# A FFN–mixer–FFN layer on one core: plain last chunk by token block, x normalised while the modulation's weights load

## The chip, the core and the metric

The kernel runs on one core of a Trainium2 chip. The metric is the device time of one execution in microseconds (us); the time before is the median of three runs. The profile is one execution recorded by the hardware profiler. The engines are called PE (TensorE: matmuls; PEld: its weight loads), DVE (VectorE), ACT (ScalarE), POOL (GpSimd) and SP, whose queue issues all DMAs of this kernel in order. PSUM is the memory that PE writes, SBUF the one that all engines read, and DRAM lies off the core.

## The reference

One layer over 1024 latent tokens `x` and 256 context tokens `ctx`, width 1024. The two streams have modulations of their own, from `c` and `c_ctx`.

```python
def rmsnorm(x, g):
    n = x * lax.rsqrt(jnp.mean(x * x, axis=-1, keepdims=True) + EPS)
    return n * g

def swiglu(y, w_in, w_out):
    gate, up = jnp.split(y @ w_in, 2, axis=-1)
    return (jax.nn.silu(gate) * up) @ w_out

m_x = (silu(c) @ w_ada + b_ada).reshape(9, 1024)          # m_c from c_ctx
x = x + 0.5 * m_x[2] * swiglu(rmsnorm(x, g1) * (1 + m_x[1]) + m_x[0], ff1_in, ff1_out)
h = h + 0.5 * m_c[2] * swiglu(rmsnorm(h, g1) * (1 + m_c[1]) + m_c[0], ff1_in, ff1_out)
# mixer: gated linear attention (GLA) and a gated MLP (gMLP) share one input and one output projection;
# the latent scans start from the context's states
x = x + m_x[5] * mix_x
x = x + 0.5 * m_x[8] * swiglu(rmsnorm(x, g3) * (1 + m_x[7]) + m_x[6], ff2_in, ff2_out)
return rmsnorm(x, final_g)
```

The hidden width of an FFN is 2816, that is 22 tiles of 128.

## The kernel before

All tensors stand transposed: channels on the 128 partitions, tokens along the free axis. `x[k][tb]` is channel tile k (8 of them) of token block tb: blocks 0 and 1 have 512 latent tokens each, block 2 is the context with 256. Every product of a big matmul is three matmuls, since both operands are split into a high part and the rest (hi by ACT, lo by DVE or POOL): hi·hi, hi·lo, lo·hi.

**An FFN.** The products for the latent tokens use a Strassen–Winograd scheme of two by two: seven products (numbered 1, 2, 5, 7, 6, 3, 4) in place of eight, over token block by half of the contraction by gate/up (or by halves of the output). The scheme needs sums of the operands: those of the weights are made in `unit` for each job, those of the moving side in `combos` (four DVE subtractions and five hi/lo pairs for each tile beside the two plain ones). `winograd` runs a list of jobs. There are 22 hidden jobs of 84 matmuls (128x512), and in the first FFN 48 more of 128x256 for the context. Each pair of hidden jobs gives one hidden tensor in seven forms, which go to DRAM (`hd`, the context's to `hc`). Then 24 output jobs come in chunks of 1, 2, 2, 2, 2, 2 pairs; a job of a two-pair chunk has 42 matmuls (and 24 of 128x256 for the context). Each chunk's result is added by DVE to SBUF accumulators; the product shared by three quarters gathers in `us` and is folded in once. The last chunk adds the gate and the residual (`finish`), squares on ACT and adds the squares on DVE (`tail`, L463), and leaves the context's last products (`later`) to the end.

**Around the FFNs.** `rstd` sums squares over the channels: ACT squares, DVE adds eight tiles up (L314), PE sums over the partitions with a vector of ones (`col_sums`, L265), 12 small DVE operations make 1/rms, and PE spreads it over the partitions (`spread`, L288). At the start the modulation's first two of nine parts are row products with PE (L205, 16 weight tiles of 512 KB), copied by ACT and turned into columns (L215); the other seven are dot products on DVE (L168) from loads `ar<-in_wb`. After the first FFN the norm waits for both token blocks and is then applied block by block; the mixer's input projection (L356) follows. After the mixer's output projection `wo`, `done2(tb)` norms a block and prepares the second FFN's moving operands. After the second FFN both blocks are normed together, scaled (L1412) and stored.

**The order.** A scheduler at build time lays each engine's instructions in one order; only the weight preparations carry a higher priority. On the chip every engine works its own list in order and waits for the others by semaphores. Buffers come from rings by tag (`raw` 2, `ar` 2, `w` 6, `m` 8, `d` 32, `h` 7; PSUM `pg` 3, `po` 3, `pn` 2), so a load also waits until an older tile of its ring is free.

## Time and profile before

| | |
|---|---|
| median of 3 runs | 2185.55 us (2184.21 to 2193.85) |
| profiled execution | 2185.07 us, of which the span 2183.3 |
| PE busy | 2016.1 us, 92% of the span |
| DVE busy | 1541.3 us, 71% |
| ACT, POOL busy | 832.8 us, 420.2 us |
| mean granted PE clock | 0.957 |

The span is what the profiler sees from the first to the last instruction; 1.8 us lie outside. PE is busy in most of the span, so what the other stretches cost is read from the waits in front of PE's instructions. The stages in order: start up to about 90 us, hidden jobs of the first FFN to 643, its output jobs to 927, mixer to 1475, second FFN to 2153, end. "Granted clock" is the share of the full TensorE clock (1.0 is 2.4 GHz, 0.5 is 1.2 GHz).

### The profile page before, as it was taken

Reading aid. Unit: us, or ns where it says so; the run is one execution under the profiler, and the core shown is the slowest. Engines: PE = TensorE matmul, PEld = TensorE weight load, DVE = VectorE, ACT = ScalarE, POOL = GpSimd, SP = SyncE. Lnnn points to the kernel's source line nnn. Section 1 sums busy time; section 2 is a strip of 40 time slices with the busy share of each in tenths; the row PEclk is TensorE's granted clock in tenths of the full one; section 3 lists DMA queues with packets and bytes.
Section 4 is the critical chain, followed back from the end, with each engine's and each line's share of the span. In section 5 each row is a group of like instructions: output and inputs, shape, how many; then the busy total and the mean of one; then the engine's idle time right before and its main releaser. Section 6 shows DMA issues by size and latency. Waiting matters only on the chain.

```text
span 2183.3 us, 28555 instructions
## 1 busy us (share of the span) xinstructions
PE 2016.1 (92%) x10820; PEld 1669.9 (76%) x10820; DVE 1541.3 (71%) x2543; ACT 832.8 (38%) x1322; POOL 420.2 (19%) x245
## 2 busy tenths in 40 slices
PE   6799999999999999879999998596999999989995
PEld 2678888888887888757788876474888888867884
DVE  3976665656675779979888376679677786755587
ACT  3633333333342121256556345226344443441222
POOL 0000000000025666422210010200000000065762
PEclk9799999999999999979999899798999999999997
DMA  7033333333369687411111125551444343568852
GB/s 282 24 111 131 116 135 126 121 116 116 116 252 390 251 299 279 156 63 54 40 60 53 35 88 214 205 164 39 164 157 161 118 180 127 194 258 340 307 198 77
DMA packets 115881, 344.86 MB, mean 158 GB/s; under 512 B 12960, under 2 KB 15904, under 8 KB 115744
## 3 DMA queue, kind: packets, MB, share of 16 engines
q1 hardware_dynamic: 115744, 343.04, 42.7%
q8 instruction: 85, 1.39, 0.3%
q14 instruction: 52, 0.43, 0.1%
HBM read 237.60 MB, written 105.38 MB: 157 GB/s over the span
## 4 chain that ended last, share of the span: by engine, by line
PE 67%; DVE 17%; DMA 6%; issue 6%; ACT 3%; POOL 1%; SPq 0%; POOLq 0%; DVEq 0%; ACTq 0%
PE c L479 15%; PE a L479 14%; PE f L479 14%; PE b L479 7%; DVE acc L741 4%; DVE acc L512 2%; DMA ar<-in_wb 2%; PE gc L526 2%; PE gc L525 2%; PE gc L524 2%; DMA hc<-hd 2%; PE row L205 1%; DVE junk L168 1%; DVE hl L430 1%; DVE x L625 1%
## 5 line engine op out<-in xcount | busy, mean ns | idle before, releaser
L384 POOL TENSOR_TENSOR gl<-raw,gh 128x1024 fp32r<-128x1024 f32 x22 | 54.1, 2460 | 1168.8 <-ACT gh L389 1157.2
L168 DVE SCALAR_TENSOR_TENSOR junk<-ar,cr 128x512 bf16<-128x512 f32 x160 | 112.6, 704 | 63.7 <-DMA ar<-in_wb 45.1
L389 ACT ACTIVATE gh<-raw 128x1024 fp32r<-128x1024 f32 x66 | 70.0, 1060 | 197.7 <-PE c L479 70.7
L393 ACT ACTIVATE sh<-s 128x1024 fp32r<-128x1024 f32 x66 | 69.8, 1057 | 167.9 <-PE a L479 94.8
L429 ACT ACTIVATE hl<-g 128x512 fp32r<-128x512 f32 x110 | 67.5, 625 | 159.5 <-DVE g L512 152.0
L479 PE MATMUL f<-hl,uh 128*128 128x512 f32 x528 | 126.8, 389 | 0.0
L479 PE MATMUL c<-hl,sh 128*128 128x512 f32 x352 | 112.5, 397 | 11.8 <-ACT hl L429 9.2
L479 PE MATMUL a<-hl,gh 128*128 128x512 f32 x352 | 114.1, 402 | 8.1 <-ACT hl L429 5.6
L479 PEld LDWEIGHTS f<-hl,uh 128*128 128x128 f32 x528 | 99.1, 188 | 20.6
L479 PE MATMUL b<-hl,gh 128*128 128x512 f32 x352 | 112.0, 395 | 1.0 <-ACT hl L429 1.0
L479 PE MATMUL a<-hl,sh 128*128 128x512 f32 x352 | 110.6, 395 | 1.0 <-ACT g L552 1.0
L479 PE MATMUL f<-hl,th 128*128 128x512 f32 x352 | 110.2, 390 | 1.3 <-ACT hl L429 1.3
L479 PE MATMUL c<-hl,th 128*128 128x512 f32 x352 | 109.0, 391 | 0.1
L741 DVE SCALAR_TENSOR_TENSOR acc<-z,par,acc 128x945 f32<-128x945 f32 (+2 forms) x64 | 95.5, 1512 | 12.3 <-ACT acc L763 11.3
L430 DVE TENSOR_TENSOR hl<-g,hl 128x512 fp32r<-128x512 f32 x110 | 76.7, 712 | 32.5 <-ACT hl L429 32.5
L512 DVE TENSOR_TENSOR u<-c,u 128x512 f32<-128x512 f32 x44 | 30.3, 688 | 96.3 <-ACT u L562 96.3
L142 POOL TENSOR_TENSOR wl<-raw,wh 128x1024 fp32r<-128x1024 f32 x20 | 51.2, 2567 | 241.5 <-ACT wh L141 241.3
L479 PEld LDWEIGHTS c<-hl,sh 128*128 128x128 f32 x352 | 67.1, 191 | 27.5 <-ACT hl L429 9.8
L384 DVE TENSOR_TENSOR sl<-s,sh 128x1024 fp32r<-128x1024 f32 x44 | 53.8, 1224 | 45.7 <-PE gc L525 21.9
L479 PEld LDWEIGHTS a<-hl,gh 128*128 128x128 f32 x352 | 67.0, 194 | 22.3 <-ACT hl L429 6.1
L356 PE MATMUL wo<-ah,wo 128*128 128x512 f32 x128 | 52.1, 408 | 30.0 <-DVE x L1322 28.1
L479 PEld LDWEIGHTS a<-hl,sh 128*128 128x128 f32 x352 | 67.2, 191 | 16.0 <-ACT g L552 1.3
(330 smaller groups left out, 6073.2 us busy)
## 6 DMA issues: line engine op xcount, KB each, us to landing
hd<-hl SPq DMA_DIRECT2D x154, 512.0 KB, 3.6
hc<-hd SPq DMA_DIRECT2D x154, 512.0 KB, 7.7
ar<-in_wb SPq DMA_DIRECT2D x112, 256.0 KB, 3.1
raw<-in_ff1i SPq DMA_DIRECT2D x44, 512.0 KB, 3.9
raw<-in_ff2i SPq DMA_DIRECT2D x44, 512.0 KB, 4.4
raw<-in_ff1o SPq DMA_DIRECT2D x22, 512.0 KB, 5.8
raw<-in_ff2o SPq DMA_DIRECT2D x22, 512.0 KB, 5.1
raw<-in_wa SPq DMA_DIRECT2D x16, 512.0 KB, 10.0
```

What stands on the lines that cost most here:

```text
L142: eng.tensor_tensor(out=lo[:, :n], in0=src[:, :n], in1=hi[:, :n].bitcast(F32), op=ALU.subtract)
L168: i = nc.vector.scalar_tensor_tensor(out=self.junk, in0=w, scalar=1.0, in1=cbc[j], op0=ALU.mult, op1=ALU.mult, accum_out=acc[:, h, dt, j:j ...
L356: m = nc.tensor.matmul(out, a_, xh[k], start=(i == 0), stop=False)
L384: sub = lambda o, x, y: eng.tensor_tensor(out=o, in0=x, in1=y, op=ALU.subtract)
L389: nc.scalar.activation(gh, g, AF.Copy)
L393: nc.scalar.activation(sh, s, AF.Copy)
L429: nc.scalar.activation(t[:, :512], src, AF.Copy)
L430: nc.vector.tensor_tensor(out=t[:, 512:], in0=src, in1=t[:, :512].bitcast(F32), op=ALU.subtract)
L479: mm = lambda x, y, start, stop: nc.tensor.matmul(ps, x, y, start=start, stop=stop, skip_group_check=more)
L512: tt = lambda eng, o, x, y, op: eng.tensor_tensor(out=o, in0=x, in1=y, op=op)
L524: nc.tensor.matmul(ps, hi[:, c], mh, start=i == 0, stop=False)
L741: self.nc.vector.scalar_tensor_tensor(out=o, in0=zv[:, r0 + dr:r1 + dr, c0 + dc:c1 + dc], scalar=self.par[:, tap:tap + 1], in1=o, op0=ALU. ...
```

## The change

- **Start.** `ada_first` writes its four row products into one PSUM bank, at the partitions 0, 32, 64 and 96, that is by four column groups of PE, where before there were four banks at partition 0. All loads of x and the context are issued first, then the first two tiles of FFN weights, then the 16 modulation weights. `scaled()` squares on ACT and sums all eight squared tiles on PE (80 matmuls of 128x1 in place of 10, with no adds on DVE), then multiplies x by 1/rms. The copies of the rows into SBUF (two on ACT, two on DVE) stand behind the last of these multiplications. Shift and scale are then one ACT operation.
- **First hidden job.** It is plain: eight products (96 matmuls) by token block (`block0`, `block1`). Its weights `w0` need no sums (`halves`); in the second FFN they are prepared within the mixer (`weights2`).
- **Last output chunk.** It is plain and goes by token block (`last`): 8 tiles of 12 matmuls for block 0, then for block 1, then 8 of 12 (128x256) for the context. The last two pairs are stored in four forms, not seven. `done(tb)` norms each block as soon as its tiles are through; in the second FFN it also writes the block's output.
- Accumulators, x and its copy in DRAM (`xe`) are laid out by pair of channel tiles and token block.

```diff
-    def ada_first(self):
-        pr = [[self.po("row") for _ in range(2)], [self.pg("row") for _ in range(2)]]
+    def ada_first(self, order):
+        nc = self.nc
+        pr = self.pg("row")
         for i in range(NK):
             for ch in range(2):
-                self.ada_rows(self.a["wa"][ch], pr[ch], i)
+                wt = self.load(self.a["wa"][ch, i], tag="d")
+                for h in range(2):
+                    g = 32 * (2 * ch + h)
+                    nc.tensor.matmul(pr[g:g + 2], self.sc[:, i, :], wt[:, h * 512:h * 512 + 512],
+                                     start=(i == 0), stop=(i == NK - 1))
+        order = order()
+        row = self.h("row")
+        pts = [self.po("cols"), self.pg("cols"), self.po("cols"), self.pg("cols")]
         for ch in (1, 0):
-            self.ada_cols(ch, pr[ch])
+            for h in range(2):
+                q = 2 * ch + h
+                r = slice(32 * q, 32 * q + 2)
+                i = nc.scalar.activation(row[r], pr[r], AF.Copy) if h else nc.vector.tensor_copy(row[r], pr[r])
+                self.after(order, i)
+                for dt in range(4):
+                    nc.tensor.matmul(pts[q][:, 2 * dt:2 * dt + 2], row[r, dt * P:(dt + 1) * P], self.ident[r, r],
+                                     start=True, stop=True)
+                c = C_BADA + 8 * ch + 4 * h
+                nc.vector.tensor_tensor(
+                    out=self.mods[:, ch, 4 * h:4 * h + 4], in0=pts[q][:, :8].rearrange("p (k j) -> p k j", j=2),
+                    in1=self.par[:, c:c + 4].unsqueeze(2).to_broadcast([P, 4, 2]), op=ALU.add)
...
+    def halves(self, src, eng, new):
+        nc = self.nc
+        r = {}
+        for x, (i, j) in zip(src, ((1, 2), (0, 4))):
+            x = self.load(x)
+            hi, lo = new("vh", F32R), new("vl", F32R)
+            with self.tc.high_priority():
+                nc.scalar.activation(hi, x, AF.Copy)
+                eng.tensor_tensor(out=lo, in0=x, in1=hi.bitcast(F32), op=ALU.subtract)
+            r[i], r[j] = (hi[:, :512], lo[:, :512]), (hi[:, 512:], lo[:, 512:])
+        return r
...
+    def right_scaled(self, coef, mov):
+        nc = self.nc
+        A = coef[0]
+        na = self.const([P, NK], "na")
+        nc.vector.tensor_scalar(out=na, in0=A[:, :, 0], scalar1=-1.0, scalar2=None, op0=ALU.mult)
+        x = self.x
+        ds = []
+        for k in range(4):
+            ds.append(self.h("dx"))
+            nc.vector.tensor_tensor(out=ds[k], in0=x[k][0], in1=x[k][1], op=ALU.subtract)
...
+        for k in range(4):
+            for i, kk in ((1, k), (2, k + 4)):
+                self.shift(x[kk][0], coef, kk)
+                self.right_op(mov, i, k, x[kk][0])
...
+        plain.block0()
         first(0)
+        plain.block1()
...
+            def block0(s):
+                w = s.w()
+                s.pq = layer.w("pq")
+                a, b = layer.pg("a"), layer.po("b")
+                for ps, (i, j), c in ((a, (1, 2), 0), (b, (0, 4), 512)):
+                    plain(ps, rows(w, (i,)), mov[1])
+                    nc.scalar.activation(s.pq[:, c:c + 512], ps, AF.Copy)
+                    plain(ps, rows(w, (j,)), mov[2], True)
+                s.g0 = layer.h("g0")
+                nc.scalar.activation(s.g0, a, AF.Silu)
+                tt(nc.vector, s.g0, s.g0, b, ALU.mult)
+                if yc:
+                    s.ctx(0)
+                    s.ctx(1)
...
+            def block1(s):
+                w = s.w()
+                c, f = layer.pg("c"), layer.po("f")
+                for ps, rs in ((c, (1, 2)), (f, (0, 4))):
+                    plain(ps, rows(w, rs), mov[5] + mov[3])
...
+                    if pair >= pairs0:
+                        out(5, b12)
+                        out(7, b22)
+                        return
...
+                if s.fold:
+                    finish(s.m, 0)
...
+                if s.fold:
+                    fold_u(m + 4, 0)
+                    finish(m + 4, 0)
...
+        def more(x, ps, dt, j):
+            nc.vector.scalar_tensor_tensor(out=x, in0=ps, scalar=gates()[:, dt, j:j + 1], in1=x,
+                                           op0=ALU.mult, op1=ALU.add)
...
+        def finish(dt, tb):
+            if (dt // 2, tb) not in xt:
+                xt[dt // 2, tb] = load_x(dt // 2, tb)
+            self.x[dt][tb] = xt[dt // 2, tb][:, dt % 2 * 512:dt % 2 * 512 + 512]
+            more(self.x[dt][tb], xsum(dt, tb), dt, 0)
...
+        def last():
+            kd = CHUNKS[-1]
+            ws = [self.halves(w2[NFO - kd + q], nc.gpsimd, (self.w, self.m)[q % 2 == 0]) for q in range(kd)]
+            tiles = [(q * (4 // kd) + m, i, ws[q], m * kd * P) for q in range(kd) for m in range(4 // kd)
+                     for i in range(2)]
+            parts = lambda w, i, col: [(*w[r], slice(col + k * P, col + k * P + P)) for r in ((1, 2), (0, 4))[i]
+                                       for k in range(kd)]
+            for tb in range(2):
+                right = []
+                for i in ((1, 2), (5, 7))[tb]:
+                    for pair in range(pairs0, NF // 2):
+                        t = self.d("hc", F32R)
+                        nc.sync.dma_start(t.bitcast(F32), hd[pair, names.index(i)])
+                        right.append((t[:, :512], t[:, 512:]))
+                for m, i, w, col in tiles:
+                    dt = m + 4 * i
+                    ps = self.po("o") if i else self.pg("o")
+                    plain(ps, parts(w, i, col), right)
+                    more(self.x[dt][tb], ps, dt, 0)
+                    tail(dt, tb)
+                    if tb == 0:
+                        fold_u(dt, 1)
+                        finish(dt, 1)
+                    elif yc:
+                        finish_c(dt)
+                done(tb)
+            if yc:
+                cs = []
+                for pair in range(pairs0, NF // 2):
+                    t = self.m("cc", F32R)
+                    nc.sync.dma_start(t.bitcast(F32), hc[pair])
+                    cs.append(t)
+                right = [(t[:, h:h + 256], t[:, h + 256:h + 512]) for h in (0, 512) for t in cs]
+                for m, i, w, col in tiles:
+                    dt = m + 4 * i
+                    if i == 0:
+                        pc = self.po("oc")
+                    ps = pc[:, i * 256:i * 256 + 256]
+                    plain(ps, parts(w, i, col), right)
+                    more(self.x[dt][2], ps, dt, 1)
+                done(2)
...
+        weights()
...
-        self.load_x(0, new)
-        self.ada_first()
-        self.load_x(1, new)
-        self.load_x(2, [self.m])
-        rs = [self.rstd(part(0)), self.rstd(part(1)), self.rstd(part(2))]
...
+        for tb in range(3):
+            self.load_x(tb, new if tb < 2 else [self.m])
+        w0 = self.halves(a["ff1i"][0], nc.vector, self.w)
+        y = ({}, {})
+        def scaled():
+            for tb in range(3):
+                n = TBS[tb][1]
+                sqs = []
+                for k in range(NK):
+                    c = k * n % 1024
+                    if c == 0:
+                        sq = self.d("sq")
+                    sqs.append(sq[:, c:c + n])
+                    nc.scalar.activation(sqs[k], self.x[k][tb], AF.Square)
+                st = self.pn("st")
+                for t in range(n // P):
+                    for k in range(NK):
+                        nc.tensor.matmul(st[:, t:t + 1], sqs[k][:, t * P:(t + 1) * P], self.ones[:, 0:1],
+                                         start=(k == 0), stop=(k == NK - 1))
+                bc = self.spread(self.rstd_cols([st], n, 1.0 / 1024.0, None, st), n // P)
+                for k in range(NK):
+                    i = nc.vector.tensor_tensor(out=self.x[k][tb], in0=self.x[k][tb], in1=bc[:, :n], op=ALU.mult)
+            return i
+        self.ada_first(scaled)
...
+            hi, lo = y[0][2][k], y[1][2][k]
+            x = self.x[k][2]
+            self.shift(x, c1, k, 1)
+            nc.scalar.activation(hi, x, AF.Copy)
+            nc.vector.tensor_tensor(out=lo, in0=x, in1=hi.bitcast(F32), op=ALU.subtract)
+        self.right_scaled(c1, mov)
...
+        def done1(tb):
+            if "c2" not in late:
+                late["c2"] = self.norm_coef(3, C_N2, 2, "2")
+            self.alloc_y(y2, tb)
+            r = self.rstd(part(2)) if tb == 2 else self.rstd_cols([accs[tb]], 512, 1.0 / 1024.0)
+            self.norm(part(tb), late["c2"], y2, r, pool=True)
...
-        r = self.rstd_cols([accs[0], accs[1]], 512, 1.0 / 1024.0)
-        bcs = [self.spread(r[:, 4 * tb:4 * tb + 4], 4) for tb in range(2)]
...
+        def done2b(tb):
+            bc = self.spread(self.rstd_cols([accs[tb]], 512, 1.0 / 1024.0), 4)
+            b0 = self.h("bc")
+            nc.scalar.activation(b0, bc, AF.Copy)
+            for k in range(NK):
+                g = self.par[:, C_FG + k:C_FG + k + 1]
                 o = self.h("out")
-                if tb == 0 and k % 4 != 3:
-                    nc.scalar.activation(o, self.x[k][0], AF.Identity, scale=g)
+                if tb and k % 3 == 2:
+                    nc.scalar.activation(o, self.x[k][tb], AF.Identity, scale=g)
                     nc.gpsimd.tensor_tensor(out=o, in0=o, in1=b0, op=ALU.mult)
                 else:
-                    nc.vector.scalar_tensor_tensor(out=o, in0=self.x[k][tb], scalar=g, in1=bcs[tb],
+                    nc.vector.scalar_tensor_tensor(out=o, in0=self.x[k][tb], scalar=g, in1=bc,
                                                    op0=ALU.mult, op1=ALU.mult)
                 nc.sync.dma_start(a["out"][k, :, tb * 512:tb * 512 + 512], o)
```

The scheduler lays out the changed program anew. PE at the start of the program, before: `row` are the modulation's rows, `st` the sums of squares, `cols` the rows as columns, `bc` the spread 1/rms, `a` and `b` the first FFN products.

```order
L205 MATMUL row_87<-raw_90,sc 2x512
L265 MATMUL st_215<-ones,acc_192 128x1 x4
L205 MATMUL row_88<-raw_94,sc 2x512
...
L215 MATMUL cols_155<-ident,row_154 128x2 x4
L265 MATMUL st_256<-ones,acc_233 128x1 x4
L265 MATMUL st_297<-ones,acc_274 128x1 x2
L288 MATMUL bc_315<-ident,r_220 128x128 x4
L479 MATMUL a_506<-hl_336,gh_512 128x512
```

The same place in the changed kernel (`row` is now one bank; `st_187`, `st_258`, `st_327` belong to blocks 0, 1 and the context):

```order
L213 MATMUL row_110<-raw_151,sc 2x512 x2
L292 MATMUL bc_233<-ident,r_220 128x128 x4
L1504 MATMUL st_258<-ones,sq_246 128x1 x2
L213 MATMUL row_110<-raw_155,sc 2x512 x2
...
L292 MATMUL bc_304<-ident,r_291 128x128 x4
L1504 MATMUL st_327<-ones,sq_317 128x1 x4
...
L292 MATMUL bc_357<-ident,r_344 128x128 x2
L225 MATMUL cols_371<-ident,row_368 128x2 x4
```

The row products and the sums of squares alternate, and all three norms stand ahead of the modulation's columns. PE at the end of the first FFN, before: `oc` is the context's output product, `z` and `ogu` the mixer's.

```order
L526 MATMUL oc_7588<-cc_7116,uh_7363 128x256
L265 MATMUL st_7620<-ones,acc_7310 128x1 x4
L265 MATMUL st_7620<-ones,acc_7312 128x1 x4
L288 MATMUL bc_7650<-ident,r_7629 128x128 x4
L288 MATMUL bc_7699<-ident,r_7629 128x128 x4
L356 MATMUL z_7892<-y_7642,wh_7854 128x512
```

In the changed kernel (`o` are the plain chunk's tiles; `hc_7130` belongs to block 0, `hc_7360` to block 1):

```order
L609 MATMUL o_7272<-hc_7130,vl_7121 128x512
L269 MATMUL st_7301<-ones,acc_7146 128x1 x4
L292 MATMUL bc_7319<-ident,r_7306 128x128 x4
L609 MATMUL o_7368<-hc_7360,vh_7102 128x512 x2
L609 MATMUL o_7368<-hc_7360,vl_7103 128x512
```

Block 0's norm now stands between the two blocks' products, with no matmul between its two steps. PE at the end of the second FFN in the changed kernel (before, the last `f` was followed by eight `st` and eight `bc`, as above):

```order
L609 MATMUL o_17178<-hc_17139,vl_16900 128x512
L269 MATMUL st_17088<-ones,acc_16943 128x1 x4
L609 MATMUL o_17178<-hc_17141,vh_16899 128x512 x2
...
L609 MATMUL o_17229<-hc_17141,vh_16917 128x512
L292 MATMUL bc_17106<-ident,r_17093 128x128 x4
L609 MATMUL o_17229<-hc_17141,vh_16917 128x512
...
L609 MATMUL o_17263<-hc_17143,vl_16918 128x512
L269 MATMUL st_17280<-ones,acc_17159 128x1 x4
L292 MATMUL bc_17298<-ident,r_17285 128x128 x4
```

Here block 0's sums and spread stand within block 1's products, 30 matmuls into them and later, and only block 1's norm is left behind the last product.

## Rows read from the trace of the kernel before

**Rows 1.** The page: busy time by engine, share of the span and instructions

```profile
PE 2016.1 (92%) x10820; PEld 1669.9 (76%) x10820; DVE 1541.3 (71%) x2543; ACT 832.8 (38%) x1322; POOL 420.2 (19%) x245
```

**Rows 2.** Windows: length, then busy us (xinstructions) by engine, clock, DMA, GB/s

```profile
50.00:75.00 25.00, 13.32 (x40) 10.54 (x41) 21.57 (x57) 13.93 (x26) 0.00 (x0) 0.52 0.14 43
75.00:100.00 25.00, 16.20 (x88) 14.36 (x87) 23.33 (x43) 15.67 (x28) 0.00 (x0) 0.80 0.07 22
100.00:125.00 25.00, 22.59 (x107) 18.14 (x106) 24.36 (x41) 13.41 (x24) 0.00 (x0) 0.87 0.16 49
200.00:225.00 25.00, 25.00 (x135) 21.67 (x135) 20.06 (x32) 11.82 (x19) 0.00 (x0) 1.00 0.49 182
...
1700.00:1725.00 25.00, 25.00 (x112) 20.67 (x112) 22.89 (x35) 10.48 (x18) 0.00 (x0) 1.00 0.49 185
```

**Rows 3.** PE's timeline at the start: start, duration, idle before and its releaser

```profile
16.43 27.49 PE L205 MATMUL row<-raw,sc 128*2 128x512 f32 x60
...
85.31 0.55 PE L524 MATMUL gc<-y,gh 128*128 128x256 f32 x1 [7.79 <-ACT x L440]
```

**Rows 4.** DVE's timeline at the start: the modulation is complete

```profile
48.69 0.17 DVE L154 TENSOR_TENSOR mods<-cols,par 128x16 f32<-128x16 f32 x1
```

**Rows 5.** SP's timeline: the issue of DMAs, at the start and in the mixer

```profile
4.02 16.05 SPq L131 DMA_DIRECT2D raw<-in_wa  x16
...
1334.81 16.20 SPq L166 DMA_DIRECT2D ar<-in_wb  x5
```

**Rows 6.** The page's DMA issues: KB each, us from issue to landing

```profile
raw<-in_wa SPq DMA_DIRECT2D x16, 512.0 KB, 10.0
```

**Rows 7.** PE's timeline in the mixer: small fp32 matmuls, and the wait of wo

```profile
1181.43 1.09 PE L1005 MATMUL ds<-vc,kt 128*64 128x128 f32 x16
...
1235.69 0.95 PE L265 MATMUL st<-ones,sq 128*128 128x1 f32 x8
...
1385.39 0.80 PE L356 MATMUL wo<-ah,wo 128*128 128x512 f32 x1 [23.28 <-DVE x L1322]
```

**Rows 8.** PE's timeline around the first FFN's last chunk and the mixer's first products

```profile
899.71 1.22 PE L479 MATMUL f<-hc,th 128*128 128x512 f32 x2 [5.77 <-ACT th L396]
...
927.24 0.28 PE L526 MATMUL oc<-cc,uh 128*128 128x256 f32 x1
938.61 3.58 PE L265 MATMUL st<-ones,acc 128*128 128x1 f32 x16 [11.10 <-DVE acc L463]
944.66 3.65 PE L288 MATMUL bc<-ident,r 128*128 128x128 f32 x16 [2.48 <-DVE r L255]
...
952.20 0.80 PE L358 MATMUL z<-y,wh 128*128 128x512 f32 x1 [2.90 <-DVE y L334]
```

**Rows 9.** PE's timeline from the mixer's last product into the second FFN

```profile
1475.20 1.05 PE L288 MATMUL bc<-ident,r 128*128 128x128 f32 x8
...
1501.00 0.80 PE L479 MATMUL c<-hl,sh 128*128 128x512 f32 x1 [9.21 <-ACT hl L429]
```

**Rows 10.** PE's timeline where the second FFN ends

```profile
2143.88 0.74 PE L479 MATMUL c<-hc,sh 128*128 128x512 f32 x2 [1.96 <-DVE acc L512]
...
2151.59 1.52 PE L479 MATMUL f<-hc,uh 128*128 128x512 f32 x6
2160.00 3.54 PE L265 MATMUL st<-ones,acc 128*128 128x1 f32 x16 [6.88 <-DVE acc L463]
2166.10 3.75 PE L288 MATMUL bc<-ident,r 128*128 128x128 f32 x16 [2.56 <-DVE r L255]
```

**Rows 11.** DVE's timeline where the second FFN ends

```profile
2157.35 3.10 DVE L463 TENSOR_TENSOR acc<-acc,sq 128x512 f32<-128x512 f32 x5
2163.58 0.17 DVE L279 TENSOR_SCALAR r<-st 128x8 f32<-128x8 f32 x1 [3.12 <-PE st L265]
...
2169.89 2.06 DVE L1412 SCALAR_TENSOR_TENSOR out<-x,par,bc 128x512 f32<-128x512 f32 x3 [3.94 <-PE bc L288]
```

**Rows 12.** ACT's timeline at the start: hi copies of the moving operands

```profile
69.71 2.17 ACT L429 ACTIVATE hl<-x 128x512 fp32r<-128x512 f32 x4
```

274 lines of the change are left out of this document (133 added, 141 removed).

## The prediction

> **What bounds the kernel now.** I read the page's busy times first, then the windows, then the timeline of PE wherever it waits, and last what the releasing engine did there. PE is busy for 92% of the span [rows 1]; in the steady stretches of both FFNs it never waits and its clock is 1.0 [rows 2]. There a 128x512 matmul costs 25/112 = 0.223 us. Faster helpers can gain nothing in those stretches, and more matmuls cost their full price. The change adds matmuls: per FFN 12 for the first hidden job (96 for 84) and 24 for the last chunk (192 for 168), 36 x 0.223 = 8.0 us, so 16 us in all. What it can win lies in five places where PE waits:
> - The start. The windows from 50 to 125 us hold 20 + 76 + 107 FFN matmuls (40, 88 and 107 less 20 of the norms' first and 12 of a later spread), while the steady first FFN has 135 in 25 us. That is 37.6 us of work, so the kernel stands as if full pace had begun at 125 - 37.6 = 87.4 us [rows 2]. The modulation is complete only at 48.7 [rows 4], and later PE waits for ACT's x [rows 3].
> - The end of the first FFN: 5.8 us before a job of the last chunk, then 24.7 us between the last context product (done at 927.5) and the mixer's steady products (952.2), with waits for DVE's sums, for r and for y [rows 8].
> - The start of the second FFN: full pace about 30 us after the mixer's last product, with one wait of 9.2 us for block 1's operands [rows 9].
> - The end: the last product is done at 2153.1, the span ends at 2183.3, so 30.2 us of tail; before it four waits for DVE's accumulators sum to 3.7 us, the longest 1.96 [rows 10, 11].
> - wo's wait of 23.3 us in the mixer [rows 7].
>
> **The start, term by term.** Before, the row products took 27.49 us for 60 records, two records each, so 0.92 us a product and 29 us for 32; PE, not the loads, bound them [rows 3]. Now 80 sums of squares come beside them. One is two records; eight records took 0.95 us at full clock [rows 7] and sixteen 3.54 us where the clock was low [rows 10], so 0.24 or 0.44 us a sum, 19 or 35 us in all, against 10 sums before. The ten spreads cost 0.23 to 0.47 us each (sixteen records in 3.75 us at the low clock, [rows 10]), 2 to 5 us. What two column groups of row products do at once the trace doesn't show for this shape; the nearest row is the scan's `ds`, whose neighbouring matmuls write different halves of the columns: 16 records of 128 columns in 1.09 us, 0.068 a record, where a one-column record takes 0.119 [rows 7]. So the rows cost 15 us (two at once) to 29 us (one after the other). Loads: the 16 weights now follow 12 other tiles; at an issue pace of 16.05/16 = 1.0 us [rows 5] and 10 us to landing [rows 6] the last is there at about 2 + 28 + 10 = 40 us. PE can start on squares at about 8 us. At full clock without overlap it is through at 8 + 29 + 19 + 3 = 59; with overlap at 45; at the low clock at 8 + 29 + 35 + 5 = 77.
>
> Behind that stand, in series, the context's r (2.5 us from sum to spread, [rows 10]), its spread, eight multiplications of 256 columns, the row copies with four subtractions between them on DVE (0.62 us each, [rows 11]), the columns and the bias: 12 us; and about 4 us in which PE has to wait for the first two blocks' r. Modulation complete: 75 us, with bounds of 60 and 93. From there ACT must shift and copy (0.54 us a step, [rows 12]) 16 tiles and the context's eight, where before the shift of x alone was left; but the plain first job offers 21 us of products on the first operands. I count 16 us until full pace. 75 + 16 + 2.7 (12 more matmuls) = 94 against 87.4: **-7 us**, bounds +8 (60 us) and -25 (93 us). What is gained on DVE (no adds of squares) is hidden by the longer chain.
>
> **End of the first FFN.** The old waits of 5.8 and 24.7 us go [rows 8]. What is late next: block 0's norm now stands between the two blocks' products with nothing between its steps (the order shows it). Its chain after the last tile is gate 0.7, square 0.6, add 0.6, four sums at 0.44, r 2.5, four spreads at 0.47 [rows 10, 11], together 8 us, and 0.5 for hand-overs. Block 1's tensors are queued on SP behind block 0's spills, which wait for the same gate: 8.5 to 10.5 us. Block 1's norm is covered by the context's 96 products, the context's by the mixer's. 24 more matmuls cost 5.4. 5.8 + 24.7 - 5.4 - 9 = **+16 us**, bounds +8 (another stall of the same size before the mixer) and +20 (the stall mostly hidden).
>
> **Start of the second FFN.** The plain job puts 96 products, 21 us, on operands that need only one block each; between the two blocks' spreads and behind the second there is now more to do, so the wait of 9.2 us [rows 9] and some 4 us of gaps ahead of it are covered; 2.7 for the 12 matmuls: **+11 us**, bounds +4 and +14. Its weights are ready early, at the price of four POOL operations and two loads in the mixer, where POOL is idle.
>
> **End of the second FFN.** Block 0's norm is inside block 1's products, which have 30 matmuls (6.7 us) between sums and gate. Behind the last product remains the same 8.5 us chain for one block, then eight output tiles where sixteen took from 2169.9 to 2183.3 [rows 11], half of it 6.7, and a copy: 16.5 us. A tile of block 0 has four DVE operations (0.62 to 0.75 us, 2.8 us) for 12 matmuls (2.7): one more us. 30.2 + 3.7 - 16.5 - 5.4 - 1 = **+11 us**, bounds +7 and +14.
>
> **Hidden to output.** The last pair has three hi/lo pairs and four subtractions fewer on DVE, seven operations at 0.62 us, where PE waits: up to 4.3 us each time. I take **+2 us** twice, bounds 0 and +4.
>
> **The mixer.** Its products are the same. The loads of the modulation's sixth part stand ahead of x's in the new order, which may shorten wo's wait [rows 7] or lengthen it: **0**, bounds -10 and +10.
>
> **Sum.** -7 + 16 + 11 + 11 + 4 = 35 us. The profiled execution took 2185.07 us (span 2183.3 and 1.8 outside), half a us under the median, so 2185 - 35 = **2150 us**.
>
> **Rivals.**
> 1. The start is bound by the loads. Row products overlap in pairs, sums at full clock hide in their gaps: PE is through at 45 us, the modulation complete at 60, full pace at 79, +8 in place of -7; with a few us of the mixer's wait, 2130 us. For it: `ds` [rows 7], and a clock of 1.0 while rows ran. Against it: the two norms' chains in which PE waits. The Trainium skill (TensorEngine Tiling (Array Packing), Instruction Overhead) says that a matmul with one column takes as long as one with 60, which would make the 80 sums next to nothing and give the same 2130 us; the trace doesn't agree, a one-column sum takes 0.24 us, as long as 512 columns in the FFN [rows 2, 7].
> 2. The start is slow: sums at the low clock, rows one after the other. Modulation complete at 93, start -25: 2150 + 18 = 2168 us. For it: the clock of 0.52 in the window of the old norms [rows 2].
> 3. The waits only move: block 0's norm stalls PE at both last chunks as the old tail did, so the two ends bring +5 and +3 in place of +16 and +11, and the second FFN's start +4: 2150 + 26 = 2176 us. Against it: the order has 30 products ahead of the gate in the second FFN.
> 4. Slower. SP issues in order, and x's tiles, wo's weights and the second FFN's first streamed weights (its second job's) stand behind the modulation loads of the mixer, 42 of them from about 1331 us on. Each waits for DVE to free one of two buffers; in one stretch five took 16.2 us, 3.24 each [rows 5], which would put the last at 1331 + 136 = 1467, just in time for the mixer's end at 1475. The change has put more DVE work (the first block's operands) beside them. At 5 us each the last comes at 1541, 50 us after the second FFN's full pace in my sum: 2200 us. It decides from about 4.1 us a load, and makes the kernel slower than before from about 4.9.
>
> **How the numbers follow.** Forecast 0.58 (2135 to 2165), rival 1 0.12, rival 2 0.14, rival 3 0.09, rival 4 0.07. About 0.5%, 11 us, is what a measurement of this kernel can tell from no change. Faster by more: 0.58 + 0.12 + 0.14 = 0.84; within it: 0.09; slower: 0.07. The range from 2126 to 2175 holds the forecast, rivals 1 and 2 and leaves out 3 and 4.
>
> **What would show it.** In the new profile: the modulation's bias at 70 to 80 us and full pace in the windows from about 95; one stall of 8 to 11 us between the two blocks' output tiles of the first FFN and none over 4 us before the mixer's products; no wait over 5 us after the mixer's last product; from the last product to the end 16 to 18 us; wo's wait between 13 and 33 us. I'd be wrong if the modulation comes after 90 us, if PE waits again behind block 1's or the context's products, or if SP's loads in the mixer take over 4 us each.

## The result, and the profile after

The changed kernel takes 2163.84 us (median of 4 runs, 2155.83 to 2170.16); the kernel before takes 2187.28 us beside it (4 runs). The ratio is 0.9887, with an interval of 0.9843 to 0.9931: 23 us faster, 1.1%. The forecast of 2150 was right in direction and 14 us too good. The profiled execution took 2167.33 us, of which the span is 2165.6, and its mean granted clock is 0.959.

The page's line of busy times, against [rows 1]:

```profile
PE 2047.7 (95%) x11032; PEld 1712.3 (79%) x11032; DVE 1479.1 (68%) x2466; ACT 815.8 (38%) x1298; POOL 387.6 (18%) x217
```

PE is busy for 32 us longer and the span is 17.7 us shorter, so some 50 us of waiting are gone. To see where, I marked the same points in PE's timeline of every run, each by the start of a product: the last product of each FFN part, the third gate product of the mixer, and the first and last product of `wo`. The differences, in us (e1 to e12 are the experiments below):

| stage | before | after | e1 | e4 | e9 | e12 |
|---|---|---|---|---|---|---|
| start to the first FFN's last hidden product | 639.6 | 650.4 | 627.1 | 640.0 | 634.3 | 620.9 |
| to the mixer's third gate product, some 35 us into the mixer | 341.8 | 331.4 | 328.2 | 327.5 | 340.3 | 318.5 |
| from there to the first `wo` product | 360.9 | 370.2 | 362.2 | 361.9 | 369.7 | 366.8 |
| `wo`, first to last | 132.6 | 112.8 | 114.0 | 115.2 | 113.0 | 113.6 |
| to the second FFN's last hidden product | 450.5 | 449.7 | 449.3 | 458.6 | 457.2 | 449.6 |
| to its last output product | 227.3 | 230.8 | 230.8 | 229.5 | 229.2 | 228.6 |
| tail to the end of the span | 30.6 | 20.3 | 20.0 | 20.1 | 30.6 | 20.8 |

The start lost 10.9 us, the first FFN's end gained 10.5, the mixer gained 10.5 in all (+19.8 at `wo`, -9.3 ahead of it), the second FFN's start 0.8 and its end 6.8. The forecast had -7, +18, 0, +11 and +13: the largest gain stands where I had put none.

The start in PE's timeline, to be held against [rows 3] (columns: start, duration, instruction, count, idle time before and its releaser):

```profile
10.87 7.51 PE L1504 MATMUL st<-ones,sq 128*128 128x1 f32 x34 [0.17 <-ACT sq L1500]
21.74 1.87 PE L213 MATMUL row<-raw,sc 128*2 128x512 f32 x4 [3.36 <-DMA raw<-in_wa]
23.54 1.01 PE L1504 MATMUL st<-ones,sq 128*128 128x1 f32 x4
...
33.16 5.30 PE L213 MATMUL row<-raw,sc 128*2 128x512 f32 x24
...
42.36 1.50 PE L1504 MATMUL st<-ones,sq 128*128 128x1 f32 x12
...
52.20 5.28 PE L1504 MATMUL st<-ones,sq 128*128 128x1 f32 x24
60.01 2.04 PE L292 MATMUL bc<-ident,r 128*128 128x128 f32 x8 [2.52 <-DVE r L259]
61.84 6.83 PE L1504 MATMUL st<-ones,sq 128*128 128x1 f32 x32
...
75.91 2.74 PE L225 MATMUL cols<-ident,row 2*128 2x2 f32 x16 [3.54 <-DVE row L222]
...
89.31 0.58 PE L609 MATMUL gc<-y,vh 128*128 128x256 f32 x1 [7.43 <-ACT y L1519]
```

The row products cost 0.22 us a record in their long row, half of the 27.49/60 of [rows 3]. The squares' sums (`st`, two records each) cost 0.44 to 0.55 us a sum up to 33 us, 0.43 to 0.44 after 52, and 0.25 only near 42; 56 records of them stand between the last row product, at 52, and the last spread, at 71. The windows of the same stretch (length; busy us and count by engine; granted clock; DMA share; GB/s):

```profile
38.00:45.00 7.00, 7.00 (x47) 3.97 (x43) 5.33 (x9) 1.06 (x1) 0.00 (x0) 1.00 0.66 265
45.00:57.00 12.00, 12.00 (x51) 8.55 (x50) 0.84 (x2) 0.00 (x0) 0.00 (x0) 0.52 0.00 0
57.00:93.00 36.00, 19.27 (x94) 18.40 (x93) 18.95 (x57) 12.93 (x24) 0.00 (x0) 0.50 0.00 1
```

From 45 us the granted clock is at the lower level (1.2 GHz), though PE is busy in every microsecond from 38 to 57, with sums and the last row products. The modulation is complete at 81.92, against 48.69 before [rows 4].

DVE's row for it, and the second FFN's start on DVE:

```profile
81.92 0.17 DVE L228 TENSOR_TENSOR mods<-cols,par 128x8 f32<-128x8 f32 x1 [0.71 <-PE cols L225]
...
1466.59 0.69 DVE L387 TENSOR_TENSOR s<-raw 128x512 f32<-128x512 f32 x1 [2.14 <-DMA raw<-in_ff2i]
...
1471.65 5.35 DVE L513 SCALAR_TENSOR_TENSOR x<-x,A,bc 128x512 f32<-128x512 f32 x8
```

and PE at the first FFN's end, the second FFN's start and the last tail, beside [rows 8 to 10]:

```profile
912.64 1.87 PE L269 MATMUL st<-ones,acc 128*128 128x1 f32 x8 [3.93 <-DVE acc L544]
916.94 2.08 PE L292 MATMUL bc<-ident,r 128*128 128x128 f32 x8 [2.43 <-DVE r L259]
...
1474.38 0.79 PE L609 MATMUL a<-hl,vh 128*128 128x512 f32 x1 [8.28 <-ACT hl L446]
...
2149.40 1.84 PE L269 MATMUL st<-ones,acc 128*128 128x1 f32 x8 [3.73 <-DVE acc L544]
2153.76 2.04 PE L292 MATMUL bc<-ident,r 128*128 128x128 f32 x8 [2.52 <-DVE r L259]
```

The 11.10 us wait of [rows 8] is gone and one stall between the two blocks stands in its place, as forecast. The wait of 9.21 us at the second FFN's start [rows 9] became one of 8.28, in front of block 0's first product and not block 1's: DVE first takes job 1's weights (L387), which land late, and scales block 0 (L513) only 6.6 us after PE's last `wo` product at 1465.0.

### The profile page after: what moved, and what is told of

Its sections match the earlier page's. It is cut to its first block, busy times and chain, and to the rows that moved or that the text cites. A ratio compares the mean times of both kernels' runs of the same rounds, so it can differ in the third digit from the quotient of the medians.

```text
span 2165.6 us, 28734 instructions
## 1 busy us (share of the span) xinstructions
PE 2047.7 (95%) x11032; PEld 1712.3 (79%) x11032; DVE 1479.1 (68%) x2466; ACT 815.8 (38%) x1298; POOL 387.6 (18%) x217
## 4 chain that ended last, share of the span: by engine, by line
PE 72%; DVE 14%; DMA 7%; ACT 3%; issue 3%; POOL 1%; SPq 1%; DVEq 0%; ACTq 0%; POOLq 0%
PE c L561 13%; PE a L561 13%; PE f L561 13%; PE b L561 7%; PE gc L609 6%; DMA ar<-in_wb 3%; DVE acc L895 3%; PE o L609 3%; PE oc L609 2%; DVE acc L597 1%; DVE junk L169 1%; DMA hc<-hd 1%; DVE x L790 1%; PE st L1504 1%; PE bc L292 1%
## 5 line engine op out<-in xcount | busy, mean ns | idle before, releaser
L387 POOL TENSOR_TENSOR s<-raw 128x512 f32<-128x512 f32 x18 | 23.7, 1318 | 1142.0 <-DMA cc<-hc 619.0
L393 ACT ACTIVATE gh<-raw 128x1024 fp32r<-128x1024 f32 x60 | 63.5, 1059 | 174.5 <-PE c L561 54.4
L561 PEld LDWEIGHTS f<-hl,uh 128*128 128x128 f32 x504 | 94.6, 188 | 19.6
L561 PE MATMUL f<-hl,th 128*128 128x512 f32 x336 | 103.6, 389 | 1.8 <-ACT th L400 1.8
L561 PE MATMUL a<-hl,gh 128*128 128x512 f32 x336 | 105.1, 392 | 0.0
L561 PE MATMUL c<-hl,sh 128*128 128x512 f32 x336 | 104.6, 392 | 0.0
L561 PE MATMUL b<-hl,gh 128*128 128x512 f32 x336 | 104.2, 390 | 0.0
L561 PE MATMUL a<-hl,sh 128*128 128x512 f32 x336 | 104.0, 390 | 0.0
L895 DVE SCALAR_TENSOR_TENSOR acc<-z,par,acc 128x945 f32<-128x945 f32 (+2 forms) x64 | 91.1, 1446 | 13.1 <-ACT acc L917 12.1
L609 PE MATMUL o<-hc,vh 128*128 128x512 f32 x256 | 80.8, 397 | 0.4 <-DVE acc L597 0.4
L561 PEld LDWEIGHTS f<-hl,th 128*128 128x128 f32 x336 | 63.0, 188 | 15.3 <-ACT th L400 2.3
L597 DVE TENSOR_TENSOR g<-b,g 128x512 f32<-128x512 f32 x42 | 28.9, 688 | 66.1 <-PE b L561 66.1
```

The source lines that it names most:

```text
L387: add = lambda o, x, y: eng.tensor_tensor(out=o, in0=x, in1=y, op=ALU.add)
L393: nc.scalar.activation(gh, g, AF.Copy)
L561: mm = lambda x, y, start, stop: nc.tensor.matmul(ps, x, y, start=start, stop=stop, skip_group_check=more)
L597: tt = lambda eng, o, x, y, op: eng.tensor_tensor(out=o, in0=x, in1=y, op=op)
L609: mm = lambda x, y, a, b: nc.tensor.matmul(ps, x, y, start=a, stop=b, skip_group_check=more)
L895: self.nc.vector.scalar_tensor_tensor(out=o, in0=zv[:, r0 + dr:r1 + dr, c0 + dc:c1 + dc], scalar=self.par[:, tap:tap + 1], in1=o, op0=ALU. ...
```

## The experiments

All of them compute the whole reference. Ratios are to the kernel before, run beside them.

**e1: the squares are added on DVE again.** One sum for a tile row in place of eight; the rest as after.

```
-   sqs.append(...); activation(sqs[k], x[k][tb], Square)
-   for t in range(n // P):
-       for k in range(NK): matmul(st[:, t:t+1], sqs[k][...], ones)
+   activation(sq, x[k][tb], Square); vector.tensor_tensor(acc, acc, sq, add)
+   self.col_sums(st, 0, acc, n)
```

> The changed kernel, but the squares of the start are added up on DVE as before (7 adds a block, then 10 sums on PE in place of 80). Theory S (the 80 one-column sums, 0.43 us each at the low clock, stand between the row products and the norms on PE and set the start): the rows end when the last weights land, at 40 to 42 us, the modulation is complete at 46 to 54 (82 in the changed kernel), first FFN product at 55 to 62 (89), the whole 25 to 32 us faster than the changed kernel, 2132 to 2139 us. Theory O (the order of the row copies behind the last multiplication by 1/rms, three norms in series, sets it): the modulation comes only some 10 us sooner, at 70 to 74, the whole at about 2154. Theory D (DVE becomes the bound, its adds delay the multiplications): within 5 us of the changed kernel.

2134.85 us (0.976, 0.9727 to 0.9794): 29 us faster than after. Its PE timeline:

```profile
21.70 4.76 PE L213 MATMUL row<-raw,sc 128*2 128x512 f32 x16 [5.96 <-DMA raw<-in_wa]
...
28.00 1.03 PE L213 MATMUL row<-raw,sc 128*2 128x512 f32 x4 [0.25 <-DMA raw<-in_wa]
...
48.19 1.19 PE L292 MATMUL bc<-ident,r 128*128 128x128 f32 x4 [5.67 <-DVE r L259]
...
66.33 0.58 PE L609 MATMUL gc<-y,vh 128*128 128x256 f32 x1 [7.43 <-ACT y L1517]
```

Four records of a weight take 1.03 us and PE then waits for the next load: the rows are bound by the loads, and the first FFN product comes at 66.3 in place of 89.3. That is 23.0 us for the 70 sums taken away, and the first stage shows 23.3.

**e2: the row copies are not ordered behind the scaling.** `self.after(order, i)` is taken out of after.

> The changed kernel, but the row copies are not ordered behind the last multiplication by 1/rms. Theory S (PE's sums set the start): the columns come at about 56 us in place of 76, but the context's norm, which the first FFN products on PE's list need, still ends at 77, so the first FFN product comes at 82 to 87 us (89) and the whole is 2 to 7 us faster than the changed kernel, 2157 to 2162. Theory O (the order sets it): first FFN product at about 70, the whole 15 to 20 us faster, about 2145.

2153.62 us (0.9845, 0.9802 to 0.9887). The modulation is complete at 59.4 in place of 81.9 and the first FFN product comes at 75.97, 13 us earlier than after and between the two expectations. The median falls by 10 us, with intervals that still overlap. So the order costs too: it held the modulation back behind norms that the sums had made late.

**e3 and e4: the old start, and the last chunk alone.** e3 is after with the start of before; e4 has the first hidden job of before too, so it is before with the plain last chunk alone.

```
 e3:  ada_first, norm_coef, right_ops(0), norm, right_ops(1) as before;  w0 = halves(ff1i[0]); block0, block1
 e4:  the same, and w0 = None: the first job by Winograd's seven products
```

> The changed kernel with the start of the kernel before (four banks of rows, norms by DVE's adds, loads in the old order); the plain first job and the plain last chunk stay. The end of the hidden jobs, less 2.7 us for 12 matmuls, was 8 us later in the changed kernel than before; if that is all the start's doing, this one is 8 to 11 us faster than the changed kernel, 2153 to 2156 us. If the plain first job is what keeps the first FFN late (its products wait for both halves of block 0), it is within 3 us of the changed kernel.

> The kernel before with the plain last chunk by token block alone: old start, and a first job in seven products in both FFNs. Measured in the changed kernel against before: first FFN's output part 9 us won net of its 24 matmuls, second FFN's 4 us, tail included. If these hold by themselves and the mixer is unchanged (wo's wait of 23 us returns), it is 13 us faster than before, 2174 us. If the mixer's 15 us also come from the last chunk (another order on SP's queue), it is 25 to 30 us faster, about 2160. If the plain first job is worth its matmuls in the second FFN (3.6 us), this one lies that much above the kernel with the old start plus 5.4.

e3 takes 2148.34 us (0.9816, 0.9779 to 0.9854), e4 2154.03 (0.9849, 0.9815 to 0.9884). By medians the parts add up so: last chunk alone 2187 to 2154, plain first job to 2148, new start back up to 2164. But these differences hold more than the parts. The 33 us of e4 are not all the chunk's own: its `wo` stage fell to 115.2 as well, though nothing there was edited, and e3 has a long one again (128.8). The stage that the start ends in is cleaner: 640.0 in e4, 631.5 in e3, 650.4 in after. There the plain first job gains 8.5 us for all its 12 more matmuls, and the new start costs 18.9, each to some 5 us (last section).

**e5: the modulation's loads of the mixer, moved early.** Before, with the dot products of its sixth part placed ahead of the scan's second half.

```
-   g1 = self.gla(1);  q1 = [...]
    for h in range(2): for dt in range(NK): self.ada_part(5, dt, h, ...)
+   g1 = self.gla(1);  q1 = [...]
    for ch in (6, 7): ...
```

> The kernel before with one edit: in the mixer the dot products of the modulation's sixth part stand before the second direction of the scan, which moves all 48 modulation loads of the mixer ahead of x's, og's and wo's loads on SP. Theory M (wo's wait of 23.3 us is the modulation's late sixth part, held up because its last loads stood behind x's and og's on SP's in-order queue): wo's wait falls under 5 us and the waits for x within wo's products go too, the whole 20 to 32 us faster than the kernel before, 2157 to 2169 us. Theory X (the plain last chunk freed buffers in the mixer, and that removed the wait): wo's wait stays above 15 us here, the whole within 8 us of the kernel before. Rival: DVE is needed by the scan, the dot products delay it by their 34 us: slower than before.

2182.84 us, ratio 0.9995 (0.9984 to 1.0007): no change. `wo` fell to 95.8 us, and the stage ahead of it grew from 360.9 to 398.5. The wait did depend on these loads, and DVE's time for the dot products was only moved.

**e6: the row products in four banks at partition 0** (else e1), so in one column group as before.

```
-   pr = self.pg("row");   matmul(pr[32*(2*ch+h) : ... + 2], ...)
+   pr = [[po("row"), po("row")], [pg("row"), pg("row")]];   matmul(pr[ch][h][:2], ...)
```

> The kernel of e1 (squares added on DVE) with the row products written to four banks at partition 0, as before the change. Theory C (neighbouring row products in different column groups run at the same time; one pair took 1.03 us there, against 0.92 us for each alone): the 32 products take 29 us, from 21.7 to 51, nine us longer than the loads; the modulation and the first FFN product come 7 to 10 us later than in e1, the whole 2141 to 2146. Rival (the loads bound the rows anyway): within 3 us of e1, 2135.

2156.39 us (0.9869, 0.9846 to 0.9892), 21.5 us slower than e1. Its rows:

```profile
21.90 14.40 PE L212 MATMUL row<-raw,sc 128*2 128x512 f32 x28 [5.95 <-DMA raw<-in_wa]
37.10 15.61 PE L212 MATMUL row<-raw,sc 128*2 128x512 f32 x36
...
69.77 1.19 PE L291 MATMUL bc<-ident,r 128*128 128x128 f32 x4 [6.65 <-DVE r L258]
...
93.47 0.58 PE L608 MATMUL gc<-y,vh 128*128 128x256 f32 x1 [15.51 <-ACT y L1516]
```

64 records in 30.0 us; in the later row 0.43 each (15.61/36), where the four column groups take 0.22 (5.30/24): two to one, and PE instead of the loads is the bound. The Trainium skill ("TensorE: Matmul & The Clock Gate", Part 3: Packing small matmuls) says that products which write different groups of 32 output partitions run at once; the trace agrees, though four groups bring no more than the factor of two. The first FFN product is 27 us later than in e1 and the rows explain about 10 of them (52.7 against 42.5 for the end of the last), as expected; the scheduler also put two norms behind the rows, and the waits for these (6.65 and 15.51 us above) are the rest.

**e7: block 0's norm within block 1's products** (else e1): both blocks' tensors of the last chunk are loaded ahead, and `done(0)` comes after three of block 1's tiles.

```
+   rights = [loads of block 0, loads of block 1]
    for tb in range(2): for ti, tile in enumerate(tiles):
+       if tb and ti == 3: done(0)
-       ... done(tb) after each block
```

> The kernel of e1 with the last chunk's tensors of both blocks loaded ahead, and block 0's norm asked for after the first three tiles of block 1. Theory B (the stall of 7.2 us between the two blocks in the first FFN, and the lower clock behind it, is only the place of the norm on PE's list): the stall falls under 1.5 us, the whole 7 to 11 us faster than e1, 2124 to 2128. Rival (block 1's tensors or DVE's gate are late anyway, or block 1's norm now comes too late for the mixer): under 3 us.

2134.28 us (0.9766, 0.974 to 0.9792), as e1. The stall is gone, and the 11 us went to another wait:

```profile
888.35 0.95 PE L269 MATMUL st<-ones,acc 128*128 128x1 f32 x8
...
1335.56 0.79 PE L360 MATMUL wo<-ah,wo 128*128 128x512 f32 x1 [10.29 <-DVE x L1482]
```

The first FFN's output part fell from 306.4 to 295.5 us, and `wo` went back from 114.0 to 128.8.

**e8: job 1's weight sums on POOL** (else e1): `lazy(w1[f], nc.gpsimd if f == 1 else nc.vector, ...)`.

> The kernel of e1 with the sums of job 1's weights on POOL in place of DVE, in both FFNs. Theory W (at the start of the second FFN DVE waits for job 1's weight load and then makes its sums before it scales block 0, 6 us behind the mixer's last product; at the first FFN's start they lie between the operands too): PE's wait of 8.7 us before the second FFN's first product falls to 3 or 4, the whole 4 to 8 us faster than e1, 2127 to 2131. Rival (POOL takes 2.5 us for each sum of 1024 columns, so job 1 comes too late): equal or up to 10 us slower.

2142.18 us (0.9811, 0.9792 to 0.983), 7 us slower than e1, with intervals that just touch. PE behind its last `wo` product, which ends at 1439.9:

```profile
1444.80 0.80 PE L561 MATMUL a<-hl,gh 128*128 128x512 f32 x1 [3.51 <-DVE x L1476]
...
1457.33 0.95 PE L269 MATMUL st<-ones,acc 128*128 128x1 f32 x8
...
1472.32 0.79 PE L609 MATMUL c<-hl,vh 128*128 128x512 f32 x1 [7.54 <-ACT hl L446]
```

The wait in front of block 0's products fell from 8.66 us in e1 to 3.51, as expected. But block 1's sums of squares now stand behind block 0's products, 17.4 us after `wo` (12.9 in e1), and block 1's first products wait 7.54 and then 2.27 us where e1 has one wait of 0.94. The stage ends even, 451.0 against 449.3: the wait moved from block 0 to block 1. By the stages most of the 7 us lies ahead, at `wo` (118.2 against 114.0) and in front of it (365.1 against 362.2).

**e9: the order of the loads in the mixer, alone.** Before, with one edit: the loads of x in the mixer stand behind the sixteenth load of the modulation's sixth part.

```
+   self.ar_load = nc.sync.dma_start(w, self.a["wb"][ch - 2, dt, ...])
+   if ch == 5: self.last5 = self.ar_load
-   nc.sync.dma_start(t, self.xd[k // 2, tb])
+   self.after(self.last5, nc.sync.dma_start(t, self.xd[k // 2, tb]))
```

> The kernel before with one order added: on SP, x's loads of the mixer stand behind the last of the 16 loads of the modulation's sixth part, and nothing else. Theory M2 (what the change won in the mixer is this order, which the scheduler happened to take there: in the changed kernel, e1, e4 and e8 the sixth part's dot products take 40 to 43 us and wo is done 113 to 118 us after its start; in before, e3 and e7 they take 56 to 66 and wo 129 to 133): wo's phase takes 113 to 118 us here too, the whole 12 to 18 us faster than before, 2168 to 2175. Rival (DVE's debt, as in e5: what is won in wo is lost ahead of it or at the second FFN's start): within 5 us of before.

2170.61 us (0.9927, 0.9899 to 0.9955): 16.3 us of the kernel before, by the interval 10 to 22, came from the order of one queue. SP's timeline in after, and then in e9, against the 5 loads in 16.20 us of [rows 5], behind which x's loads came first:

```profile
1325.77 35.54 SPq L167 DMA_DIRECT2D ar<-in_wb  x14
1361.36 0.90 SPq L1421 DMA_DIRECT2D x<-xd  x2
```

```profile
1331.22 26.93 SPq L166 DMA_DIRECT2D ar<-in_wb  x8
1359.29 0.33 SPq L1312 DMA_DIRECT2D raw<-in_wo  x1
1360.36 0.33 SPq L166 DMA_DIRECT2D ar<-in_wb  x1
1360.73 0.42 SPq L1267 DMA_DIRECT2D x<-xd  x1
```

In both the sixth part's loads run without x's between them. The modulation that `wo`'s residual wants is complete at 1365 and 1366 (DVE's `mods`), in before at 1384, and `wo` takes 113 us in place of 133. The stages show both sides of it: `wo` is 19.6 us shorter and the stretch ahead of it 8.8 us longer, almost what after has (19.8 and 9.3), and the second FFN's start takes 6.7 us more. The profiled execution is the longest of the four, and in it the three stages together bring 4 us; the gain of 16 rests on the medians.

**e10: e1 with a shorter path to the first product**: no order on the row copies, and the context's shift and hi/lo split behind block 0's.

> The kernel of e1 without the order of the row copies, and with the context's shift and split asked for after block 0's. Theory O2 (with the sums off PE, what is left of the start is the serial chain of the context's norm ahead of the columns, and the context's products ahead of block 0's): the modulation is complete at 47 to 50 us (59 in e1), the first FFN product at 52 to 57 (66), the whole 9 to 13 us faster than e1, 2122 to 2126. Rival (the gain falls to the mixer, whose dot products and loads keep their time): under 4 us.

2133.4 us (0.9753, 0.9728 to 0.9779), within 1.5 us of e1, with intervals that overlap widely. The first FFN product moved from 66.3 to 58.2 and the first stage from 627.1 to 620.7; 5.1 us, no more than the scatter of one trace, came back ahead of `wo`.

**e11: e7 and e9 together.**

> The kernel of e7 with the order of e9. If e7 came out even with e1 only because its schedule took the bad order of the sixth part's loads (wo's phase 128.8 us against 114.0), wo's phase is 113 to 118 us and the 11 us won at the first FFN's end stand: 2119 to 2125 us. If the mixer's tail is bound from elsewhere (DVE, the 48 loads with two buffers), under 5 us faster than e7, 2130 or more.

2123.7 us (0.9708, 0.9686 to 0.973). With the loads' order fixed, the 10.6 us that e7 alone did not bring are there.

**e12: e10, e7 and e9 together.**

> e10's start, e7's norm within block 1's products and e9's order in one kernel. If they add up: 11 + 11 us under e1, 2110 to 2116 us. If the mixer's tail absorbs one of them: 2120 to 2126.

2117.07 us (2115.24 to 2120.57; 0.9682, 0.966 to 0.9704): it beats both kernels, the one before by 70 us and the changed one by 47, and lies just above the range for gains that add up. It is 6.6 us under e11, which is what e10's start had saved in its own stage. In its windows full pace stands from 75 us:

```profile
60.00:75.00 15.00, 9.68 (x27) 7.03 (x26) 10.52 (x20) 15.00 (x32) 0.00 (x0) 0.56 0.00 1
75.00:100.00 25.00, 25.00 (x145) 22.10 (x145) 25.00 (x43) 16.86 (x32) 0.00 (x0) 1.00 0.18 53
```

## Why the prediction came out as it did

**The start (forecast -7, measured -10.9 in the trace): the failed step is the pace at which I let the sums run.** I counted 80 sums at 0.24 us, "at full clock without overlap", and took 0.44 as the bound of rival 2. The trace charges 0.44 in the first long row (34 records in 7.51 us) and 0.50 at 23.54, both where the windows list a clock of 1.0, and 0.43 in the 56 records (12.1 us) behind the fall of the clock. Only short stretches around 40 us have 0.25 (12 records in 1.50), the price that I had used. The early half pace isn't the sums' own: up to 31 us four row records beside them take 1.87 us, later 1.03, and in the kernel before the first four take 3.57 us, 0.89 each, against 0.46 in the 60 of [rows 3]:

```profile
11.13 3.57 PE L205 MATMUL row<-raw,sc 128*2 128x512 f32 x4 [11.13 <-DMA raw<-in_wa]
```

What causes it is open, but it stood in the trace that I had. In the same sum the rows were priced too high: four groups at once make them 0.22 us a record in their long row, 14 us for all 32 products, where I had bounds of 15 and 29 and put the 29 into the sum. So the picture was wrong twice in opposite directions: rows cheap as in rival 1, sums dear as in rival 2. The modulation came at 81.9 (forecast 75, bounds 60 and 93). e1 settles the cause: without the 70 extra sums the same start gives 23 us more. The order of the row copies, which I had in the chain, is the second link: when it alone is taken out, the first FFN product comes 13 us sooner (e2); taken out of e1, together with the context's split in front of block 0, it brings 8 us more (e10). How much of the loss against before is real is known only to some 5 us: before's own 639.6 is the longer of two lengths that the same start has shown (last section). The total of rival 2, 2168, is 4 us from the result, but not by its mechanism, for its rows stood one after the other.

I was wrong to say that the trace disagrees with the rule of the Trainium skill (TensorEngine Tiling (Array Packing), Instruction Overhead), that a matmul with one column takes as long as one with 60. The rows show just such a flat price: 0.119 us a record with one column (8 in 0.95, [rows 7]), 0.131 with 128 (8 in 1.05, [rows 9]). What failed is what I drew from it, that sums of one column would be next to nothing; 70 of them cost 29 us (e1).

**First FFN's end, with the last chunk's hidden-to-output step (forecast +18, measured +10.5).** The stall between the blocks is what I forecast: 3.93 and 2.43 us idle in the rows of after above, and e7, which hides it, gains 10.9 in that stage. The rest I had not counted. The last chunk's Winograd sums end one chunk earlier now, and DVE is late there: from 760 to 900 us PE idles for 4.7 us, where before it idled for 0.2 up to 893. The same happens in the second FFN.

The windows of that chunk in the second FFN, before and then after:

```profile
2040.00:2110.00 70.00, 70.00 (x310) 57.61 (x309) 47.93 (x70) 13.24 (x14) 51.16 (x31) 1.00 0.67 252
```

```profile
2030.00:2100.00 70.00, 64.52 (x275) 52.04 (x274) 55.02 (x73) 13.45 (x14) 43.29 (x23) 0.98 0.56 206
```

PE never waited there before and waits for 5.5 us now, with DVE 7 us busier. What makes it busier is in DVE's groups of the same two stretches, before and then after (count; busy us and mean ns of one; idle us before them):

```profile
L512 DVE TENSOR_TENSOR acc<-acc,u 128x512 f32<-128x512 f32 x10 | 11.8, 1185 | 0.3
```

```profile
L790 DVE SCALAR_TENSOR_TENSOR x<-acc,hg,x 128x512 f32<-128x512 f32 x12 | 13.1, 1101 | 0.1
L597 DVE TENSOR_TENSOR acc<-acc,u 128x512 f32<-128x512 f32 x9 | 11.4, 1277 | 0.1
```

The gates and residuals of twelve tiles (`x<-acc,hg,x`), which before came in the last chunk, are new here with 13.1 us; all the rest is 6 us less. After's DVE, POOL and PE in the middle of it:

```profile
2073.32 2.88 DVE L597 TENSOR_TENSOR acc<-acc,u 128x512 f32<-128x512 f32 x1
2076.12 0.68 DVE L597 TENSOR_TENSOR acc<-f,acc 128x512 f32<-128x512 f32 x1
2076.72 2.27 DVE L790 SCALAR_TENSOR_TENSOR x<-acc,hg,x 128x512 f32<-128x512 f32 x1
2078.92 2.82 DVE L597 TENSOR_TENSOR acc<-acc,u 128x512 f32<-128x512 f32 x1
```

```profile
2069.96 5.68 POOL L423 TENSOR_TENSOR vl<-raw,vh 128x1024 fp32r<-128x1024 f32 x2 [3.66 <-ACT vh L422]
2075.96 2.49 POOL L388 TENSOR_TENSOR sl<-s,sh 128x1024 fp32r<-128x1024 f32 x1 [0.31 <-PE c L561]
2078.41 2.78 POOL L388 TENSOR_TENSOR tl<-s,th 128x1024 fp32r<-128x1024 f32 x1
```

```profile
2082.40 0.74 PE L561 MATMUL a<-hc,sh 128*128 128x512 f32 x2 [4.09 <-DVE acc L597]
```

An `acc<-acc,u`, both of whose inputs lie in SBUF, takes 2.88 or 2.82 us beside POOL's weight sums, and all 15 of after that no POOL operation overlaps take 0.67 to 0.69; `acc<-f,acc`, with one input in PSUM, takes 0.68 even beside POOL, and so do all 136 of its kind that POOL overlaps (0.67 to 0.69). The Trainium skill ("SBUF — State Buffer", Who interferes with whom) says that a DVE operation with two inputs in SBUF contends with GpSimd's reads, and one with at most one such input, outside the 2-port modes, does not; the trace agrees on both. I had priced every such operation at 0.62 to 0.75 us. But `acc<-acc,u` paid this before as well (11.8 us for ten, 11.4 for nine now), so it is no part of the 7 us. New are the twelve operations on x, at 0.74 us each 8.9 of their 13.1 us, and the 4.2 us above that, in those that POOL overlaps. No run moved POOL's sums away, so what PE would win without the contention was not tried.

**The mixer (forecast 0, measured +10.5): the step left out.** I had seen that the new order puts the modulation's loads ahead of x's, and gave it no value but bounds of 10 each way. It is worth 16.3 us by itself (e9), and at `wo` 19.8, twice my bound; 9.3 are lost ahead of `wo`. Where the scheduler lets x's loads in between, `wo` takes 129 to 133 us (before, e3, e7), else 113 to 118 (after, e1, e2, e4, e6, e8 to e12; e5 moved more and has 95.8). e4 and e7 didn't touch the mixer and flipped it. Why 9.3 us are lost ahead of `wo` is open: e9 loses 8.8 there by the same edit of the order, but e1 and e4, with the same order of loads, have 362 there.

**The second FFN's start (forecast +11, measured +0.8): the failed step is the cover.** I let 21 us of plain products hide the 9.21 us wait, without asking when block 0's own operands are ready. They are late, since DVE serves job 1's weight sums first. e8, with those sums on POOL, shows the second half: block 0's wait falls by 5 us, and then block 1's norm isn't covered. With `wo` at 113 to 118 us the Winograd job needs 457 to 459 us for this stage (e4, e9) and the plain job 448 to 453 (after, e1, e2, e6, e8, e10 to e12), so there it wins 4 to 10 us. With the longer `wo` it wins nothing: 450.5 before, 451.0 in e3 and 450.3 in e7. And e5, with the shortest `wo`, has 451.4 by Winograd. What the job is worth hangs on what the mixer has left undone when it starts; by what path isn't shown.

**The second FFN's end, with its hidden-to-output step (forecast +13, measured +6.8).** From the end of the last product the tail took 19.9 us and not 16.5: the chain to the spread 10.1 for my 8.5, the eight output tiles 9.7 for my 8. The output part grew by 3.5 us where I had 0.7: the 24 matmuls are 5.4, and the wait of 4.09 us shown above is new.

**The rivals.** 3 (waits only move) has the FFNs' sizes better than my sum: the two ends and the second FFN's start brought 18.1 us, where it had 16 and I had 42, both with the hidden-to-output step. For the first FFN its mechanism is right too: one stall of the size that I had forecast remained, and e7 shows its 11 us. 4 didn't come: 14 loads in 35.54 us are 2.5 us each, under its 4.1 (and under 3.8, which its own "50 us" at 5 us a load would give).

**The total.** Without the mixer's 10.5 us, which I had put at 0, the trace would be 7 us faster than before and not 18, against a forecast of 35. That the total came out within 14 us of 2150 is luck: a gain that I didn't forecast stands in for four stages that all fell short.

A gain in one stage doesn't always reach the total by itself: the start's 6.4 us in e10 gave 1.5, e7's 10.9 gave 0.6. Both are there in the kernels that join them: with the queue's order fixed e11 is 10.6 us under e7, and e12 is 6.6 under e11. For e10 against e1 the intervals are too wide to say that its gain was ever lost.

## What to carry to other kernels

Price work moved onto an in-order engine at the pace that the same engine has in that stretch of the old trace, whatever clock is listed there, and check what stands behind it: 70 small matmuls between a load-bound phase and the norms cost 29 us, though DVE, where they came from, was idle enough. When a change lets a scheduler reorder a DMA queue, test the order by itself with one edit to the old kernel; here it was about two thirds of the net gain (16 of 23 us, each with an interval of 6 to 10 us on either side) and belonged to no part of the change. A saving in one stage counts only when the next wait doesn't depend on something with its own pace, so try it together with the fix of that wait before dropping it.
